# A two-layer trunk: the first layer's output projection in two parts, its memory attention three steps earlier, small matmuls in fewer groups

## The chip, the cores and the metric

The kernel runs on one core of a Trainium2 chip. TensorE (PE) multiplies matrices into PSUM, an accumulator memory of eight banks of 128 partitions x 512 fp32 values; VectorE (DVE), ScalarE (ACT) and GpSimd (POOL) do the elementwise work; DMA queues, here almost all issued by SyncE (SP), move data between device memory and the on-chip SBUF. Every engine works through its own list of instructions in order and waits on semaphores for the others. The metric is the device time of one execution in microseconds.

## The reference

One sequence of 512 tokens, model width 1024, two layers, all in float32. Each layer adds a token mixer and a memory cross-attention, which share one input and one output projection, and then a gated feed-forward block with a causal convolution of width 3:

```python
for i in range(DEPTH):
    h = rms_norm(x, attn_norm[i])
    if i % N_MIXERS == 0:
        proj = h @ w_in_diff[j]                  # 1024 -> 2560
        mix = diff_attention(q, k, v, ...)       # 6 heads of 2 x 64
    else:
        proj = h @ w_in_gla[j]
        mix = gla_attention(q, k, v, r, gate_low, ...)   # 4 heads, chunks of 64
    cross = memory_cross_attention(mem_q, mem, ...)      # 4 heads into 256 memory tokens
    x = x + jnp.concatenate([mix, cross], axis=-1) @ w_out[i]
    h = rms_norm(x, ffn_norm[i])
    x = x + conv_ffn(h, w_up[i], conv_w[i], conv_b[i], w_down[i])   # 1024 -> 5632 -> 1024
```

Differential attention normalizes queries and keys, adds a relative bias, masks by chunks, and subtracts a second softmax from the first: `w = p[:, :, 0] - lam * p[:, :, 1]`; its output is normalized per head. Memory attention normalizes the memory tokens, its queries and its keys, and is a plain softmax attention.

## The kernel before

**Products.** Every large product is made in three terms from operands split into a high and a low part (hi·hi, hi·lo, lo·hi), each a 128x128 weight against 512 columns; a 128x512 matmul follows the one before at 0.23 us. Weights come in pieces of up to 128x1024: a DMA into one of three raw buffers (`load_raw`, L208), a cast to the high part on ACT (`split_weights`, L201) and a subtraction for the low part on DVE (L202). There are five buffers each of high and low parts; `weights(key)` keeps two pieces made ahead. Activations are split in the same way by `split` (L234 on ACT, L235 on DVE), and memory-token operands too.

**Small work.** Between these run small fp32 matmuls: transposes (L170), the attention logits (L608 in the differential layer, L501 for memory) and values (L644, L534), and column sums (L342). PSUM banks are lent under four tags of two banks each: `lg` (logits, sums), `tp` (transposes), `mm` (large products), `sm` (values, second half of large products). A request for a bank waits until the last reader of its earlier use is done.

**Order.** PE's order is as written in the program. A queue `F` of large-product units stands beside it: `F.add(cost, unit)` or `gemm(...)` puts units in, `F.fill(us)` issues units for that much time, `F.need(mark)` issues all up to a mark, `F.flush()` all that is left. So the program writes the small groups and says with `F.fill` how much large work is put between them. The other engines' orders are made by a scheduler, except in the head (`with ... manual_schedule`, L351 to L425), where ACT, DVE, POOL and SP also follow the program.

**Head.** x is loaded and split in eight 128-row parts, each multiplied with the first weight piece as it arrives (L425) into four banks. At k = 6 the second piece is split (`make_piece(second)`: four casts and four subtractions), and the sums of squares are turned into r_x (`token_rsqrt`: L342 on PE, L184 on DVE, L191 and L192 on ACT, L177 to L179 on DVE). Then `halves` evacuates the four banks on ACT with the scale r_x into qs and ks (L560, L561).

**Differential layer** (`diff_layer`). `norms` makes the root-mean-square factors of qs and ks (squares L304, sums L305, multiplication L308), `prepare` transposes them (L170, evacuated at L584). A loop of 28 steps t handles unit t (head t // 4, query block t % 4) in stages one step apart: `logits(t)`, with the reduction L613, the exponentials L616 and the combination L622; `turn(t - 1)`, which transposes the weights through `tp` and copies them on ACT (L633); `values(t - 2)`. Every fourth step `finish` transposes and splits one head's output. `MemAttn` runs along it from step M0 = 12: `logits(b)` (maximum L504, exponentials L508, normalization L512 on POOL), `turn(u)` (copy on DVE, L521), `values(b)`; its `slot` picks which. `mem_kv(l)` makes a layer's memory operands, keys and values (L461, L462) and returns `operands` and `keys` (evacuation kmT at L470); that of layer 1 is made here as well, from t = 0. Two fills per step, each of `FA` = 3.0 us up to t = 13 and `FB` = 1.2 us after.

**Output projection.** `PASS` lists, for each layer, parts; each part is a list of column blocks c with the mixer rows k that it multiplies. Layer 0 has four: three inside the loop (t = 14, 20, 24), whose results `update` adds to x (L964 on DVE), and one after the loop, which also splits the new x and sums its squares (`squares`, L334 and L336) for the feed-forward block. `xT` is loaded again by `load_x` at t = 14, eight transfers of 256 KB.

**GLA layer** (`gla_layer`). Gates and decays (L795 to L802), then ten `slot`s of memory attention with `F.fill(2.4)` after each, then for each head h scores, turned keys, states and outputs with `F.fill(f)`, f = 2.5, between.

Of the kernel before, what the change touches and what calls it, by code (L numbers as in the profile page):

```python
# [22 lines left out]
NB = S // 128  # L23
# [106 lines left out]
def trunk(ctx, tc, head_d, x_t, mem_t, wpack, cols_a_d, cols_d, conv_d, gate_d, rel_bias, diff_lambda, consts, onehot, out):  # L130
# [224 lines left out]
    with tc.tile_pool(name="ini", bufs=1) as ip, tc.manual_schedule(engines={E.Activation, E.DVE, E.Pool, E.SP}):  # L355
# [50 lines left out]
        for k in range(KT):  # L406
            if k + 1 < KT:
                operands(k + 1)
            if k == 0:
                second.append(load_raw(raws[0], WTILE))  # L410
            if k == 4:
                bias_rows(rb, oh, bs)
            if k == KT - 2:
                make_piece(second)
                weights(("qk", 0))
                token_rsqrt("lg", acc[0], NB, r_x[:, 0])
                small_vectors()
                for c in range(2):
                    load(bias_d[:, 512 * c:min(512 * c + 512, 640)], bs[c])
            hi, lo = parts[k]  # L420
            terms = (xh[k], hi), (xh[k], lo), (xl[k], hi)
            todo = [(b, i) for b in range(NB) for i in range(3)]
            for b, i in sorted(todo, key=lambda bi: bi[1]) if k == 0 else todo:
                xp, w = terms[i]
                mm(first[b], xp[:, blk(b)], w, start=k == 0 and i == 0, stop=k == KT - 1 and i == 2)  # L425
# [16 lines left out]
        V.tensor_add(sq[:, 0:256], sq[:, 0:256], sq[:, 256:512])  # L442


    def mem_kv(l):
        hs, ls = [None] * KT, [None] * KT
        km = [None]

        def operands():
            if l == 0:  # L450
                mem_squares()
            km[0] = xtile().rearrange("p (b n) -> p b n", b=2)
            for k in range(KT):
                if k % 2 == 0:
                    mh, ml = split_tiles()
                c = blk(k % 2, 256)
                hs[k], ls[k] = mh[:, c], ml[:, c]
                split(hs[k], ls[k], memT[k // 2][:, c], c_mem(l, k))

        def ev(b, p):  # L460
            A.activation(km[0][:, b], p[:, :256], AF.Copy, scale=r_mem[:, b:b + 1])  # L461
            A.activation(vm[l][:, b], p[:, 256:], AF.Copy, scale=r_mem[:, b:b + 1])  # L462

        def keys():
            F.need(f"kv{l}")
            p = bank("lg")
            for hp in range(2):
                for b in range(2):
                    transpose(p[:, 256 * hp + 128 * b:256 * hp + 128 * b + 128], km[0][:, b, blk(hp)])
            A.activation(kmT[l].rearrange("p a b -> p (a b)"), p, AF.Copy, scale=c_mk(l))  # L470
        gemm(hs, ls, 2, ("kv", l), 512, ev,
             (lambda: token_rsqrt("lg", mem_acc[0], 2, r_mem)) if l == 0 else None)
        F.add(0.0, lambda: group_norm(None, km[0], 2, 4, 64))
        F.mark(f"kv{l}")
        return operands, keys


    class MemAttn:
# [36 lines left out]
        def turn(self, u):  # L515
# [5 lines left out]
            V.tensor_copy(pT, pt)  # L521
            self.live[u] = pT


# [15 lines left out]
        def slot(self, t):  # L540
            if t in (3, 5, 7, 9):
                self.values((t - 3) // 2)
            if t in (0, 2, 4, 6):
                self.logits(t // 2)
            if 0 <= t - 1 < 8:
                self.turn(t - 1)


    def diff_layer(pool, mix):
        r = r_x[:, 0]  # L550
        qm = pool.tile([128, NB, MEM], F32, name="qm", bufs=1)

# [119 lines left out]
        F.fill(1.2)  # L672
        prepare(1)
        ma = MemAttn(pool, 0, qm, mix, False)
        M0 = 12
        for t in range(28):
            if t == 0:
                project_qk(1)
                ops0, keys0 = mem_kv(0)
# [36 lines left out]
            if t % 4 == 3 and t >= 7:  # L716
                finish(t // 4 - 1)
        F.flush()


    def gla_layer(pool, mix, acc):
# [131 lines left out]
        def scores(h):  # L853
            pp = bank("lg")
            for b in range(NB):
                mm(pp[:, blk(b)], ke[:, blk(b)], qi[:, blk(b)], start=True, stop=True)
            V.copy_predicated(sv, MF.unsqueeze(1).to_broadcast([128, NB, 128]),
                              pp.rearrange("p (b n) -> p b n", b=NB))
            for b2 in range(2):
                pp = bank("lg")  # L860
                for b in (2 * b2, 2 * b2 + 1):
                    mm(pp[:, blk(b % 2, 192)], ki[:, blk(b)], qx[h][:, b], start=True, stop=True)
                pv = pp[:, :384].rearrange("p (b c n) -> p b c n", b=2, c=3)
                V.copy_predicated(
                    sv[:, 2 * b2:2 * b2 + 2].rearrange("p b (c n) -> p b c n", c=2),
                    MP.rearrange("p (c n) -> p c n", c=2).unsqueeze(1).to_broadcast([128, 2, 2, 64]), pv[:, :, 0:3:2])
                A.copy(sv[0:64, 2 * b2:2 * b2 + 2, 64:128], pv[0:64, :, 1])
                if b2 == 0:
                    F.fill(1.2)

        def turn_keys(h):
            pt = bank("tp")
# [47 lines left out]
                mix[t] = (mh, ml)  # L920
                F.fill(1.2)

        f = 2.5
        decays(0)
        F.need("qk")
        F.fill(f)
        products(0)
        F.fill(f)
        for h in range(4):
            scores(h)  # L930
            F.fill(f)
            turn_keys(h)
            if h < 3:
                decays(h + 1)
            F.fill(f)
            states(h, 0)
            F.fill(f)
            if h == 2:
                gate(0)
            outputs(h, 0)  # L940
            states(h, 1)
            if h < 3:
                products(h + 1)
            F.fill(f)
            outputs(h, 1)
            group_norm(pool, o_[h], NB, 1, 192, True)
            F.fill(f)
# [21 lines left out]
        squares(xT[n], acc, V if n == KT - 1 else eng)  # L969


    def tiles(l, part):
        cs, kk = [c for c, _ in PASS[l][part]], dict(PASS[l][part])
        if l == 0 and part == 3:
            return [2 * c + n for a in (0, 2) for n in range(2) for c in cs[a:a + 2]], kk
        return [2 * c + n for c in cs for n in range(2)], kk

    def out_proj(l, mix, part, acc):
        got = {}
        turns = cycle(("mm", "sm") if part == len(PASS[l]) - 1 else ("mm",))  # L980

        def unit(c, ks, n, i):
            if i == 0:
                if c not in got:
                    got[c] = weights(("o", l, part, c))
                got["p"] = bank(next(turns))
            p = got["p"]
            product(p, got[c], n, [mix[k] for k in ks], (i,))
            if i == len(ks) - 1:
                update(2 * c + n, p, None if acc is None else (lambda k: c_ffn(l, k)), acc, G if l else V)  # L990
        todo, kk = tiles(l, part)
        for n in todo:
            for i in range(len(kk[n // 2])):
                F.add(0.65, lambda n=n, i=i: unit(n // 2, kk[n // 2], n % 2, i))

    def ffn(pool, l, acc):
        rB = pool.tile([128, S], F32, name="rB", bufs=1)
# [1 line left out]
        for u in us:  # L999
            G.memset(u[:, 0:2], 0.0)  # L1000
        nu = [0]
        order = tiles(l, len(PASS[l]) - 1)[0]

        def up(parts, n):
            i = nu[0]
            nu[0] += 1
            p = bank("mm" if i % 4 < 2 else "sm")
            product(p, parts, n, list(zip(xh, xl)), order)
            return p, us[i % 4]

        def conv(p, u, j):
# [55 lines left out]
    for l in range(2):  # L1067
        with tc.tile_pool(name=f"at{l}", bufs=2) as pool:
            mix = [None] * 8
            if l == 0:  # L1070
                diff_layer(pool, mix)
            else:
                gla_layer(pool, mix, acc)
            acc = [None]
            out_proj(l, mix, len(PASS[l]) - 1, acc)
            F.flush()
        with tc.tile_pool(name=f"ff{l}", bufs=2) as pool:
            acc = ffn(pool, l, acc)

# [74 lines left out]
```

## Time and profile before

| quantity | value |
| --- | --- |
| runs of the kernel | 1201.24, 1201.85, 1203.02 us; median 1201.85 |
| profiled execution | 1205.09 us, span 1203.3 us, mean granted PE clock 0.997 |
| PE | 1186.3 us busy, 99% |
| DVE | 766.7 us, 64% |
| ACT | 542.4 us, 45% |
| POOL | 31.2 us, 3% |
| device memory | 112.65 MB read, 4.21 MB written, 97 GB/s over the span |

The span runs from the profile's first to its last instruction. In rows of the timeline stand the start in us, the duration, the engine with line and operation, output <- inputs, shapes, and in brackets the idle time of the engine before it with what ended it. Matmuls are pipelined: a row's duration overlaps the next row's start, so distances between starts say more than durations. In the list of costly groups stand line, engine, operation and count, then the total busy time in us and the mean in ns, then the engine's idle time before such instructions and what ended most of it; in the list of DMA issues, the count, the size of one, and the median us from issue to landing.

### The profile page before, as it was taken

Reading aid. Unit: us, or ns where it says so; the run is one execution under the profiler, and the core shown is the slowest. Engines: PE = TensorE matmul, PEld = TensorE weight load, DVE = VectorE, ACT = ScalarE, POOL = GpSimd, SP = SyncE. Lnnn points to the kernel's source line nnn. Section 1 sums busy time; section 2 is a strip of 40 time slices with the busy share of each in tenths; the row PEclk is TensorE's granted clock in tenths of the full one; section 3 lists DMA queues with packets and bytes.
Section 4 is the critical chain, followed back from the end, with each engine's and each line's share of the span. In section 5 each row is a group of like instructions: output and inputs, shape, how many; then the busy total and the mean of one; then the engine's idle time right before and its main releaser. Section 6 shows DMA issues by size and latency. Waiting matters only on the chain.

```text
span 1203.3 us, 14795 instructions
## 1 busy us (share of the span) xinstructions
PE 1186.3 (99%) x5656; PEld 967.9 (80%) x5656; DVE 766.7 (64%) x1280; ACT 542.4 (45%) x928; POOL 31.2 (3%) x45
## 2 busy tenths in 40 slices
PE   9999998999999999999999999999999999999998
PEld 7777776778888888888787788988888888888887
DVE  6567577887776533767447746768777653476741
ACT  6666666554444322434436534536544432243420
POOL 0000011000000000000020000003000000000000
PEclk9999999999999999999999999999999999999999
DMA  8333231133242322332442222143333232232231
GB/s 289 110 98 94 80 114 45 62 108 103 73 133 75 123 90 68 108 103 63 138 127 95 71 71 57 57 132 107 104 98 113 70 123 95 68 124 81 88 114 44
DMA packets 39556, 117.81 MB, mean 98 GB/s; under 512 B 4703, under 2 KB 6040, under 8 KB 39486
## 3 DMA queue, kind: packets, MB, share of 16 engines
q1 hardware_dynamic: 39342, 116.62, 30.1%
q8 instruction: 44, 0.72, 0.2%
q14 instruction: 26, 0.21, 0.1%
q10 hardware_dynamic: 144, 0.26, 0.1%
HBM read 112.65 MB, written 4.21 MB: 97 GB/s over the span
## 4 chain that ended last, share of the span: by engine, by line
PE 88%; DVE 6%; DMA 2%; ACT 2%; issue 1%; SPq 0%; DVEq 0%; ACTq 0%
PE ps_mm L269 8%; PE ps_mm L268 8%; PE ps_mm L270 8%; PE ps_sm L268 7%; PE ps_sm L269 7%; PE ps_sm L270 7%; PE ps_mm L251 5%; PE ps_mm L253 5%; PE ps_mm L252 5%; PE ps_tp L268 3%; PE ps_tp L269 3%; PE ps_tp L270 3%; PE ps_lg L269 3%; PE ps_lg L270 3%; PE ps_lg L268 3%; PE ps_tp L170 2%
## 5 line engine op out<-in xcount | busy, mean ns | idle before, releaser
L201 ACT CAST whi<-raw 128x1024 fp32r<-128x1024 f32 (+2 forms) x214 | 207.6, 977 | 247.3 <-PE ps_tp L269 133.9
L202 DVE TENSOR_TENSOR wlo<-raw,whi 128x1024 fp32r<-128x1024 f32 (+2 forms) x214 | 241.8, 1139 | 109.5 <-ACT whi L201 108.6
L268 PE MATMUL ps_mm<-xsh,whi 128*128 128x512 f32 x458 | 182.2, 398 | 0.2 <-DVE xt L964 0.2
L269 PE MATMUL ps_mm<-xsl,whi 128*128 128x512 f32 x458 | 179.1, 391 | 0.3 <-DVE xsl L235 0.2
L270 PE MATMUL ps_mm<-xsh,wlo 128*128 128x512 f32 x458 | 178.8, 390 | 0.0
L268 PE MATMUL ps_sm<-xsh,whi 128*128 128x512 f32 x374 | 145.5, 389 | 0.0
L269 PE MATMUL ps_sm<-xsl,whi 128*128 128x512 f32 x374 | 145.5, 389 | 0.0
L270 PE MATMUL ps_sm<-xsh,wlo 128*128 128x512 f32 x374 | 145.5, 389 | 0.0
L251 PE MATMUL ps_mm<-whi,xsh 128*128 128x512 f32 (+2 forms) x352 | 138.6, 394 | 1.8 <-ACT ks L561 1.7
L253 PE MATMUL ps_mm<-whi,xsl 128*128 128x512 f32 (+2 forms) x352 | 131.7, 374 | 0.3 <-DVE xsl L235 0.3
L252 PE MATMUL ps_mm<-wlo,xsh 128*128 128x512 f32 (+2 forms) x352 | 131.1, 372 | 0.0
L1014 ACT ACTIVATE cvo<-u,cv 128x512 f32<-128x512 f32 x88 | 71.6, 814 | 113.4 <-DVE u L1012 113.0
L269 PEld LDWEIGHTS ps_mm<-xsl,whi 128*128 128x128 f32 x458 | 86.3, 189 | 18.9 <-DVE xsl L235 1.5
L268 PEld LDWEIGHTS ps_mm<-xsh,whi 128*128 128x128 f32 x458 | 86.3, 188 | 18.5 <-DVE xt L964 0.9
L270 PEld LDWEIGHTS ps_mm<-xsh,wlo 128*128 128x128 f32 x458 | 86.3, 188 | 18.1
L1015 DVE SCALAR_TENSOR_TENSOR cvo<-u,cv,cvo 128x512 f32<-128x512 f32 x88 | 65.9, 749 | 31.6 <-ACT cvo L1014 31.4
L270 PEld LDWEIGHTS ps_sm<-xsh,wlo 128*128 128x128 f32 x374 | 70.2, 188 | 14.6
L269 PEld LDWEIGHTS ps_sm<-xsl,whi 128*128 128x128 f32 x374 | 70.2, 188 | 14.6
L268 PEld LDWEIGHTS ps_sm<-xsh,whi 128*128 128x128 f32 x374 | 70.2, 188 | 14.6
L251 PEld LDWEIGHTS ps_mm<-whi,xsh 128*128 128x128 f32 x352 | 66.7, 189 | 13.6 <-ACT ks L561 2.1
L253 PEld LDWEIGHTS ps_mm<-whi,xsl 128*128 128x128 f32 x352 | 66.4, 189 | 12.8 <-DVE xsl L235 0.5
L252 PEld LDWEIGHTS ps_mm<-wlo,xsh 128*128 128x128 f32 x352 | 66.7, 190 | 9.5
(257 smaller groups left out, 1767.6 us busy)
## 6 DMA issues: line engine op xcount, KB each, us to landing
raw<-in_wpack_dram SPq DMA_DIRECT2D x176, 512.0 KB, 3.5
raw<-in_wpack_dram SPq DMA_DIRECT2D x27, 256.0 KB, 3.5
xt<-in_x_t_dram SPq DMA_DIRECT2D x15, 256.0 KB, 6.0
xres<-xt SPq DMA_DIRECT2D x8, 256.0 KB, 2.8
xt<-xres SPq DMA_DIRECT2D x8, 256.0 KB, 3.1
out_dram<-xt SPq DMA_DIRECT2D x8, 256.0 KB, 2.0
bt<-bias_d SPq DMA_DIRECT2D x6, 256.0 KB, 4.1
raw<-in_wpack_dram SPq DMA_DIRECT2D x4, 384.0 KB, 3.0
```

The source lines that it names most:

```text
L170: nc.tensor.transpose(dst, src, ident[:n, :n])
L201: A.copy(hi[:, c], raw[:, c])
L202: V.tensor_sub(lo[:, c], raw[:, c], hi[:, c].bitcast(F32))
L251: mm(p, sh[k][:, blk(b)], hi, start=k == 0, stop=False)
L252: mm(p, sh[k][:, blk(b)], lo, start=False, stop=False)
L253: mm(p, sl[k][:, blk(b)], hi, start=False, stop=k == KT - 1)
L268: mm(p, hi[:, blk(n)], bh, start=i == first, stop=False)
L269: mm(p, hi[:, blk(n)], bl, start=False, stop=False)
L270: mm(p, lo[:, blk(n)], bh, start=False, stop=i == last)
L1014: A.activation(c, u[:, 2:], AF.Identity, scale=cv[l][:, 2, j:j + 1], bias=cv[l][:, 3, j:j + 1])
L1015: V.scalar_tensor_tensor(c, u[:, 1:S + 1], cv[l][:, 1, j:j + 1], c, op0=ALU.mult, op1=ALU.add)
```

## The change

- Layer 0's projection has two parts in place of four. Part 0 (rows 0, 1, 2) is queued at t = 16, part 1 (rows 3 to 7) at t = 26. Part 1 begins with the products of three output blocks without row 5, held open in three banks; the rest, with row 5, is queued after the loop, behind `finish(5)`.
- In the differential loop, the turn comes two steps and the values three steps after the logits; turns of both attentions stand together behind the logits; memory logits stand alone in mid-step; each step has two halves of one fill, 5.8, 2.6, 1.5 and 2.6 us by stages of t.
- Memory attention starts at M0 = 9; its queries' norm moves from t = 8 to t = 2, the queries from 11 to 4, the keys of layer 0 from 9 to 8. `mem_kv(1)` is created at t = 12 with a pool of its own for its split operands; its keys stay at t = 22.
- Every second copy of a memory turn in layer 0 is on ACT in place of DVE. The squares of layer 0's updates are summed on POOL in place of DVE, but for the last.
- In the head, `token_rsqrt` stands ahead of `make_piece(second)`.
- In the GLA layer, a fill of 2.5 us precedes memory attention, which has six steps with a fill of 4.0 in place of ten with 2.4; per head, both states, the next head's products and both outputs stand together, with f = 3.6.
- The feed-forward block takes its rows in plain order.

```diff
-FA, FB = 3.0, 1.2
+STEPS, FILL = (14, 19, 26), (5.8, 2.6, 1.5, 2.6)
...
-PASS = ([[(c, (0, 1)) for c in C4], [(c, (2, 3)) for c in C4], [(c, (6, 7)) for c in (0, 1)],
-         [(2, (6, 7, 4, 5)), (0, (4, 5)), (3, (6, 7, 4, 5)), (1, (4, 5))]],
+PASS = ([[(c, (0, 1, 2)) for c in C4], [(c, (3, 6, 7, 4, 5)) for c in C4]],
...
             if k == KT - 2:
+                token_rsqrt("lg", acc[0], NB, r_x[:, 0])
                 make_piece(second)
                 weights(("qk", 0))
-                token_rsqrt("lg", acc[0], NB, r_x[:, 0])
...
-            V.tensor_copy(pT, pt)
+            (V.tensor_copy if self.l or u % 2 == 0 else A.copy)(pT, pt)
...
-        M0 = 12
+        M0 = 9
         for t in range(28):
             if t == 0:
                 project_qk(1)
...
-                ops1, keys1 = mem_kv(1)
-            if t == 8:
-                ma.norm()
-            if t == 9:
-                keys0()
             if t == 2:
                 ops0()
-            if t == 11:
+                ma.norm()
+            if t == 12:
+                ops1, keys1 = mem_kv(1, pool, "mo", 8)
                 ops1()
             if t == 22:
                 keys1()
-            if t == 14:
+            if t == 16:
                 load_x(x_t)
                 out_proj(0, mix, 0, None)
-            if t in (20, 24):
-                out_proj(0, mix, t // 4 - 4, None)
-            f = FA if t < 14 else FB
-            if t == 11:
-                ma.queries()
+            if t == 26:
+                rest = out_proj(0, mix, 1, acc, 5)
+            f = FILL[bisect(STEPS, t)]
             if t < 24:
                 logits(t)
+            m = t - M0
+            if m in (4, 6, 8, 10):
+                ma.values(m // 2 - 2)
+            if 0 <= t - 3 < 24:
+                values(t - 3)
             if 0 <= t - 2 < 24:
-                values(t - 2)
-            F.fill(f)
+                turn(t - 2)
+            if 2 <= m < 10:
+                ma.turn(m - 2)
+            F.fill(f / 2)
             if t in (5, 6, 13, 14):
                 norms((t + 3) // 8, (t + 3) % 8)
-            if 0 <= t - 1 < 24:
-                turn(t - 1)
-            ma.slot(t - M0)
-            F.fill(f)
+            if t == 4:
+                ma.queries()
+            if t == 8:
+                keys0()
             if t in (7, 8, 15, 16):
                 prepare(2 * (t // 7) + (t + 1) % 8)
+            if m in (0, 2, 4, 6):
+                ma.logits(m // 2)
+            if t == 27:
+                F.flush()
+            F.fill(f / 2)
             if t % 4 == 3 and t >= 7:
                 finish(t // 4 - 1)
+        rest()
         F.flush()
...
-        for t in range(10):
-            ma.slot(t)
-            F.fill(2.4)
+        F.fill(2.5)
+        for t in range(6):
+            if 0 < t < 5:
+                ma.turn(2 * t - 2)
+                ma.turn(2 * t - 1)
+            if t > 1:
+                ma.values(t - 2)
+            if t < 4:
+                ma.logits(t)
+            F.fill(4.0)
...
+        f = 3.6
         for h in range(4):
             scores(h)
+            past_scores(h, 0)
             F.fill(f)
+            past_scores(h, 1)
             turn_keys(h)
             if h < 3:
                 decays(h + 1)
             F.fill(f)
             states(h, 0)
+            states(h, 1)
+            if h < 3:
+                products(h + 1)
             F.fill(f)
             if h == 2:
                 gate(0)
             outputs(h, 0)
-            states(h, 1)
-            if h < 3:
-                products(h + 1)
-            F.fill(f)
             outputs(h, 1)
...
-                update(2 * c + n, p, None if acc is None else (lambda k: c_ffn(l, k)), acc, G if l else V)
+                update(n, p, None if acc is None else (lambda k: c_ffn(l, k)), acc, G)
...
+        if late is None:
+            return give(units)
+        early = [u for u in units if u[0] < 4 and kk[u[0] // 2][u[1]] != late]
+        give([u for u in early if u[0] < 3])
+        return lambda: give([u for u in early if u[0] == 3] + [u for u in units if u not in early])
```

More of the change, by code (lines that the diff above doesn't have):

```diff
@@ L1 @@
 import math
+from bisect import bisect
 from collections import deque
@@ L442, in mem_squares, with mem_kv @@
         V.tensor_add(sq[:, 0:256], sq[:, 0:256], sq[:, 256:512])
-    def mem_kv(l):
+    def mem_kv(l, pool, tag, bufs):
         hs, ls = [None] * KT, [None] * KT
@@ L538, in values, with diff_layer @@
                 split(mh[:, blk(b)], ml[:, blk(b)], po[:, blk(hp)], 1.0)
[L540 to L549, printed above, removed]
+    def diff_layer(pool, mix, acc):
         r = r_x[:, 0]
@@ L678, in diff_layer @@
                 project_qk(1)
[L679 removed]
+                ops0, keys0 = mem_kv(0, xs, "xs", XS)
                 gemm(xh, xl, NB, ("v", 1), 512, lambda b, p: A.activation(
@@ L858, in scores, with past_scores @@
                               pp.rearrange("p (b n) -> p b n", b=NB))
[L859 to L869, printed above, removed]
+        def past_scores(h, b2):
+            pp = bank("lg")
+            for b in (2 * b2, 2 * b2 + 1):
+                mm(pp[:, blk(b % 2, 192)], ki[:, blk(b)], qx[h][:, b], start=True, stop=True)
+            pv = pp[:, :384].rearrange("p (b c n) -> p b c n", b=2, c=3)
+            V.copy_predicated(
+                sv[:, 2 * b2:2 * b2 + 2].rearrange("p b (c n) -> p b c n", c=2),
+                MP.rearrange("p (c n) -> p c n", c=2).unsqueeze(1).to_broadcast([128, 2, 2, 64]), pv[:, :, 0:3:2])
+            A.copy(sv[0:64, 2 * b2:2 * b2 + 2, 64:128], pv[0:64, :, 1])
         def turn_keys(h):
@@ L969, in update, with out_proj, unit @@
         squares(xT[n], acc, V if n == KT - 1 else eng)
[L972 to L982, printed above, removed]
+    def out_proj(l, mix, part, acc, late=None):
+        got, kk = {}, dict(PASS[l][part])
+        turns = cycle(("mm", "mm", "sm", "sm") if late is not None else ("mm", "sm") if acc else ("mm",))
+        def unit(n, i):
+            c, ks = n // 2, kk[n // 2]
             if i == 0:
@@ L985, in unit, with give @@
                     got[c] = weights(("o", l, part, c))
-                got["p"] = bank(next(turns))
-            p = got["p"]
-            product(p, got[c], n, [mix[k] for k in ks], (i,))
+                got["p", n] = bank(next(turns))
+            p = got["p", n]
+            product(p, got[c], n % 2, [mix[k] for k in ks], (i,))
             if i == len(ks) - 1:
-                update(2 * c + n, p, None if acc is None else (lambda k: c_ffn(l, k)), acc, G if l else V)
[L991 to L994, printed above, removed]
+                update(n, p, None if acc is None else (lambda k: c_ffn(l, k)), acc, G)
+        def give(units):
+            for u in units:
+                F.add(0.65, lambda u=u: unit(*u))
+        units = [(2 * c + n, i) for c, ks in PASS[l][part] for n in range(2) for i in range(len(ks))]
+        if late is None:
[3 more added lines that the diff above has]
+        return lambda: give([u for u in early if u[0] == 3] + [u for u in units if u not in early])
     def ffn(pool, l, acc):
@@ L1007, in up @@
             p = bank("mm" if i % 4 < 2 else "sm")
-            product(p, parts, n, list(zip(xh, xl)), order)
+            product(p, parts, n, list(zip(xh, xl)))
             return p, us[i % 4]
@@ L1069, in trunk @@
             mix = [None] * 8
+            sums, acc = acc, [None]
             if l == 0:
-                diff_layer(pool, mix)
+                diff_layer(pool, mix, acc)
             else:
[L1073 to L1076, printed above, removed]
+                gla_layer(pool, mix, sums)
+                out_proj(1, mix, len(PASS[1]) - 1, acc)
+                F.flush()
         with tc.tile_pool(name=f"ff{l}", bufs=2) as pool:
```

8 lines of the change are left out of this document (3 added, 5 removed).

## The prediction

> **What bounds the kernel now.** I read the engines' busy shares first, then PE's list of waits, then windows cut at each gap, and then the timeline round the gaps.
>
> ```profile
> span 1203.3 us, 14795 instructions
> PE 1186.3 (99%) x5656; PEld 967.9 (80%) x5656; DVE 766.7 (64%) x1280; ACT 542.4 (45%) x928; POOL 31.2 (3%) x45
> ```
>
> PE is busy for 99% of the span, and the diff leaves PE's list of 5330 programmed matmuls as it was: the same products, transposes and shapes in another order and in other banks. So no PE work can go away. What can change is the 17 us (1203.3 - 1186.3) in which PE stands still, what each restart costs, and the stretches at a lower clock. Some of this is beyond the change (the first load, the last output). The rest has names:
>
> ```profile
> PE ps_tp L170 <- DVE xt L521: 3.1, 2, 1.6
> PE ps_mm L251 <- ACT ks L561: 1.7, 1, 1.7
> PE ps_lg L501 <- DVE xt L800: 1.5, 1, 1.5
> ```
>
> These are the three largest that the change touches: what PE did, on whom it waited, microseconds in total, times, longest. The windows (length; PE busy; PEld, DVE, ACT, POOL; granted clock; DMA share; GB/s) say where they lie:
>
> ```profile
> core 0: us, PE busy (x) PEld busy (x) DVE busy (x) ACT busy (x) POOL busy (x), PEclk, DMA share, GB/s
> ...
> 110.00:180.00 70.00, 67.82 (x368) 53.33 (x367) 45.01 (x117) 43.52 (x111) 4.58 (x5) 1.00 0.25 81
> 180.00:195.00 15.00, 11.53 (x90) 8.90 (x89) 10.08 (x29) 11.11 (x30) 2.05 (x3) 1.00 0.27 79
> 195.00:199.00 4.00, 4.00 (x15) 3.23 (x15) 2.96 (x11) 2.34 (x7) 0.14 (x1) 0.57 0.02 7
> 199.00:243.00 44.00, 43.51 (x281) 33.82 (x281) 38.50 (x104) 22.84 (x67) 2.04 (x2) 1.00 0.19 59
> 243.00:272.00 29.00, 28.52 (x124) 22.27 (x123) 26.32 (x42) 16.97 (x26) 0.21 (x4) 1.00 0.36 112
> ...
> 659.00:663.00 4.00, 4.00 (x13) 2.77 (x12) 3.97 (x7) 3.94 (x11) 0.00 (x0) 0.57 0.00 0
> ```
>
> In the differential-attention loop PE idles 70.00 - 67.82 = 2.18, then 3.47, then 0.49 us: 6.1 in all. Twice the clock drops to 0.57 on average over a 4 us window: (1 - 0.57) x 4.00 = 1.7 us lost each time. Both follow a wait of 1.5 to 1.6 us (rows at 193.59 and 658.77 below). A wait costs more than the idle shown, too: in the head (below) the starts 30.08 and 32.18 lie 2.10 apart where products follow each other at 0.23, a loss of 1.87 with 1.71 shown. At about 0.1 more for each of some fourteen short waits, the loop loses 6.1 + 1.4 + 1.7 = 9.2 us.
>
> **The base.** The profiled execution took 1205.09 us, 1.8 around its span of 1203.3. It is 3.24 above the median of the runs, 1201.85. Terms below are differences made from profiled rows; I put them on the median, since nothing shows where in the span those 3.24 us lie.
>
> **The head.** `token_rsqrt` moves ahead of the four casts of the second weight piece.
>
> ```profile
> 23.92 0.95 PE L342 MATMUL ps_lg<-C,xt 128*128 128x1 f32 x8
> ```
> ```profile
> 30.04 0.26 ACT L191 ACTIVATE r_x<-ps_lg,eps 128x4 f32<-128x4 f32 x1 [1.36 <-DVE rs_v L184]
> ...
> 31.29 0.47 ACT L560 ACTIVATE qs<-ps_mm,r_x 128x256 f32<-128x256 f32 x1 [0.75 <-DMA raw<-in_wpack_dram]
> 31.66 0.47 ACT L561 ACTIVATE ks<-ps_mm,r_x 128x256 f32<-128x256 f32 x1
> ```
> ```profile
> 30.08 0.39 PE L425 MATMUL ps_sm<-whi,xsl 128*128 128x512 f32 x1
> 32.18 0.50 PE L251 MATMUL ps_mm<-whi,xsh 128*128 128x512 f32 x1 [1.71 <-ACT ks L561]
> ```
> ```profile
> L201 ACT CAST whi<-raw 128x1024 fp32r<-128x1024 f32 (+2 forms) x214 | 207.6, 977 | 247.3 <-PE ps_tp L269 133.9
> L202 DVE TENSOR_TENSOR wlo<-raw,whi 128x1024 fp32r<-128x1024 f32 (+2 forms) x214 | 241.8, 1139 | 109.5 <-ACT whi L201 108.6
> ...
> raw<-in_wpack_dram SPq DMA_DIRECT2D x176, 512.0 KB, 3.5
> raw<-in_wpack_dram SPq DMA_DIRECT2D x27, 256.0 KB, 3.5
> xt<-in_x_t_dram SPq DMA_DIRECT2D x15, 256.0 KB, 6.0
> ```
>
> The sums for r_x leave PE at 23.92 + 0.95 = 24.87, yet r_x starts only at 30.04: it stands behind the casts. Moved ahead, r_x is ready near 26.2, and if nothing else changed the evacuation that PE waits for (it ended at 31.66 + 0.47) would lie directly behind PE's last head product, 1.9 us sooner. But the order of instructions in the two built programs shows what takes its place. ACT, which runs its list in order, now has a fifth cast (the piece after the second) ahead of the first evacuation; before, that cast stood behind all eight. Its data are loaded into a raw buffer that the first subtraction of the second piece (L202) frees, and this subtraction now follows r_x: cast 1 from 25.4 to 26.4, subtraction to 27.6 (0.98 and 1.14 each), transfer issued then, landed at 27.6 + 3.5 = 31.1, fifth cast to 32.1, two evacuations 0.37 apart, the second taking 0.47: PE starts near 33.1 instead of 32.18, **+0.9**. Lower end: the cast also needs the high-half buffer that PE frees at 30.08 + 0.39, so it cannot end before 31.5, and PE starts at 32.4 or later: +0.3. Upper end: with 6.0 for the landing, as the row of x's loads has, +3.4. Idle at 33.1 is 2.6 us in place of 1.71, above the 1.5 that came before each half-clock stretch, so I add one stretch, **+1.7** (bounds 0 and 1.7). Queued behind that fifth cast are the evacuations, and behind them layer 0's first norms, which the 10 us of fill cover.
>
> The Trainium skill ("TensorE: Matmul & The Clock Gate", Part 1: The HAM clock gate) puts the drop to half rate after at least one idle window, about 3.4 us. By that a 2.6 us gap would cost no clock and the sum would be 1.7 lower; but here 1.5 to 1.6 us of idle stood ahead of both 0.57 windows, so the trace does not agree, and I go by the trace.
>
> **The differential loop.** What goes is the pair of waits in which the transposes of ks find their tp bank still held by a memory-attention turn:
>
> ```profile
> 183.15 0.60 PE L170 MATMUL ps_tp<-C,qs 128*128 128x128 f32 x4
> 185.27 0.66 PE L170 MATMUL ps_tp<-C,ks 128*128 128x128 f32 x4 [1.52 <-DVE xt L521]
> ...
> 191.38 0.60 PE L170 MATMUL ps_tp<-C,qs 128*128 128x128 f32 x4
> 193.59 0.66 PE L170 MATMUL ps_tp<-C,ks 128*128 128x128 f32 x4 [1.61 <-DVE xt L521]
> ```
> ```profile
> 180.93 1.20 DVE L308 TENSOR_TENSOR ks<-ks,rs_y 128x1024 f32<-128x1024 f32 x1
> ```
>
> With M0 = 9 and all turns placed behind the logits, these two and most of the short waits between 110 and 180 lose their place. But the same banks (two each of lg and tp) and the same in-order lists on ACT and DVE serve the new order, and I find a new wait at most steps where small groups meet: prepare(2)'s ks behind its 1.20 multiplication (1.0), logits(6) behind the memory's norm sums (0.6), logits(10) behind a cast between memory exponentials (0.4), ma.turn(1) behind finish(1)'s split of a tp bank (0.8), logits(14) (0.7), prepare(2)'s partner at t = 15 behind the 1.20 multiplication, itself behind a turn's copy (1.5), and at t = 16, where memory logits, two turns, finish(2) and prepare(3) meet: logits(16) (0.8), ma.turn(5) (0.5), qs behind an evacuation that stands behind a cast (0.8), ks behind the copy now put on ACT (0.8); logits(22) behind keys1 (0.2). The sum is 8.1. Each is bounded by 0 and by its releaser's own duration plus one cast (0.98) or multiplication: they sum to between 4 and 13. The t = 15 and 16 waits lie close enough for one half-clock stretch, 1.7. Taken: 9.8 against 9.2, **+0.6** (range -5 to +6).
>
> The four copies given to ACT and the six adds of squares given to POOL relieve DVE, which is idle often enough that this counts only in the tail. mem_kv(1) twelve steps later adds no work: its splits lie beside products. Its keys at t = 22 stand as before. `load_x` two steps later puts eight transfers of 256 KB on SP's list ahead of later weight pieces; DMA share is 0.25 and two pieces are kept ahead, so I take 0; without that cover, one landing of x, 6.0 us, less the step in between, about 2. The projection in two parts makes larger pieces (27 transfers of 256 KB become fewer), 12 fewer adds on DVE: 0 on PE.
>
> **Layer 0's tail.** Between 243 and 272 PE idles 0.48 us in five short waits, worth about 1.3 with restarts, while DVE is busy 26.32 of 29.00. The new tail holds n = 0..2 open in three banks and has twelve products of n = 3 to run while finish(5) is split, and half a dozen fewer adds on DVE. I take 0.3 left, **-1.0** (0 to -1.3; a loss if POOL's adds end late is in the second rival's range).
>
> **The GLA layer.** A fill of 2.5 now stands ahead of the memory logits.
>
> ```profile
> 658.77 1.54 PE L501 MATMUL ps_lg<-kmT,xt 64*128 64x256 f32 x6 [1.50 <-DVE xt L800]
> ```
> ```profile
> 659.81 1.28 ACT L173 ACT_TABLE_LOAD   x1
> ```
>
> The 1.50 wait and its half-clock stretch, 3.5 with the restart, are covered by 2.5 us of products. Late next are the turns, which need the exponentials behind the table load of 1.28: 1.1 remains (0.5 to 1.5). At the end one group, with less fill left for it, loses 0.3 more. Net **-2.1** (-3.0 to -0.5).
>
> **Fewer groups.** About 103 groups of small matmuls between large ones become 80 in the built order. Entering one:
>
> ```profile
> 710.29 0.39 PE L253 MATMUL ps_mm<-whi,xsl 128*128 128x512 f32 x1
> 710.52 0.60 PE L170 MATMUL ps_tp<-C,q 128*96 128x128 f32 x4
> 710.95 0.60 PE L170 MATMUL ps_tp<-C,k 128*96 128x128 f32 x4
> 711.31 0.47 PE L251 MATMUL ps_mm<-whi,xsh 128*128 128x512 f32 x1
> 711.62 0.39 PE L252 MATMUL ps_mm<-wlo,xsh 128*128 128x512 f32 x1
> ```
>
> From 710.29 to 711.62 is 1.33; two product slots of 0.23 and eight transposes at 0.43 for four leave 0.01. So a group costs 0.01 to 0.02, and 23 fewer save **-0.25** (0 to -0.5).
>
> **The sum**: 0.9 + 1.7 + 0.6 - 1.0 - 2.1 - 0.25 = -0.15; 1201.85 - 0.15 = 1201.7 us. Waits trade places.
>
> **Rivals.** (A) *The waits go and few come back: faster.* For it: the waits at 185, 193 and 658 have a definite cause that the new order removes, and fills of 2.6 us or more then lie ahead of most groups. Against it: ACT busy 11.11 of 15.00 and DVE 10.08 exactly there. With half the loop's loss (-4.6), the head at its lower end without a clock stretch (+0.3), tail and GLA as above: 1201.85 - 4.6 + 0.3 - 1.0 - 2.1 - 0.25 = 1194.2.
>
> (B) *In-order lists at t = 15 and 16: slower.* Place: ACT's weight casts and copies standing ahead of evacuations while both tp banks are held. Price: the loop's waits at their upper end of 13, with two clock stretches of 1.7 instead of one, 16.4 - 9.2 = +7.2; with the head's +2.6 and the other terms 1201.85 + 7.2 + 2.6 - 3.35 = 1208.3. It decides once two of those waits exceed 1.5 us. For it: both such waits did so before. Against: more fill between them.
>
> (C) *It does not do what it says.* The filler runs dry ahead of part 1 of the projection, so that small groups run uncovered as before and only the head's loss remains: 1201.85 + 2.6 - 0.25 = 1204.2.
>
> **Chances.** A difference under 0.2% (2.4 us) counts as none. Forecast 0.36: its own range is 1198 to 1206, so 0.22 within, 0.06 faster, 0.08 slower. A 0.31, faster. B 0.29, slower. C 0.04, half within, half slower. Faster 0.37, same 0.24, slower 0.39. A spreads from 1190 to 1199 and B from 1204 to 1214 by the ends of their terms; a tenth left out at each side, a third of A and of B, gives 1193 to 1211, and I take 1191.5 below, since the loop's own lower end (-5) lies beyond A's -4.6.
>
> **What would show it.** Right: PE's wait on ks in the head longer than 1.71; no wait of L170 on L521 over 1 us in the loop, but several of 0.5 to 1.5 at t = 15 and 16; the GLA's 1.50 gone with its 0.57 window. Wrong: the first product after the head starting before 32.2; the loop's idle under 3 or over 10 us; PE's busy time without clock stretches moving by more than 1 us.

## The result, and the profile after

The changed kernel takes 1213.53 us (median of 4 runs, 1212.01 to 1214.33), the kernel before 1202.43 (4 runs, 1201.24 to 1203.02): a ratio of 1.0092, 95% interval 1.0075 to 1.0110. It is 11.1 us slower, above the range's upper end of 1211. Its profiled execution took 1212.01 with a span of 1210.2 and a mean granted clock of 0.994, against 1205.09, 1203.3 and 0.997: only 6.9 between the two profiles. The other 4.2 us matter below.

PE's list of waits after the change (what it did, on whom it waited, total, times, longest):

```profile
PE ps_mm L251 <- ACT ks L554: 2.9, 1, 2.9
PE ps_tp L170 <- DVE ks L308: 2.3, 1, 2.3
PE ps_mm L269 <- DVE xsl L235: 2.3, 2, 1.9
PE ps_tp L170 <- ACT xt L626: 2.0, 2, 1.3
PE ps_tp L170 <- DVE xsl L235: 1.7, 3, 1.1
PE ps_tp L170 <- DVE rcd L612: 1.6, 1, 1.6
PE ps_tp L170 <- ACT xt L521: 1.5, 1, 1.5
PE ps_mm L268 <- ACT xsh L234: 1.4, 1, 1.4
```

None of the three waits that led the list before is there in its old form; these eight lines are. In order of time they are the head (2.9), the transposes of ks for `prepare(2)` (2.3), steps 15 and 16 of the loop (0.7, 1.6, 1.3, 1.5), as the third and the eighth line the last rows of the new x at the start of the feed-forward block (row 6: 0.3; row 7: 1.4 for its high part and 1.9 for its low part), and, as the longest part of the fifth line, a group of transposes at the end of the GLA layer (1.1). The windows (columns as in the prediction) show what came after the head, after `prepare(2)`, after step 15 and after row 7:

```profile
34.00:38.00 4.00, 4.00 (x12) 3.09 (x12) 2.29 (x5) 4.00 (x12) 0.00 (x0) 0.57 1.04 399
...
112.00:116.00 4.00, 4.00 (x14) 3.19 (x13) 1.49 (x7) 1.37 (x2) 0.00 (x0) 0.57 0.03 13
...
191.00:195.00 4.00, 4.00 (x17) 2.71 (x14) 2.44 (x7) 2.31 (x9) 0.80 (x2) 0.57 0.60 214
...
280.00:284.00 4.00, 4.00 (x10) 2.56 (x9) 1.77 (x3) 1.32 (x2) 0.00 (x0) 0.60 0.28 113
```

Four stretches at about half clock, 1.6 to 1.7 us lost in each, where before had two.

PE's work is the same in both, so the start of one and the same instruction tells what was lost up to it. The first product after the head starts 0.84 later than before (33.02 against 32.18), the column sums of the feed-forward block 7.86 later (279.56 against 271.70). Adding up PE's start-to-start distances less the usual distance for each shape, by stages, gives after against before: up to 45 us +2.4, 45 to 160 +3.0, 160 to 245 -0.7, 245 to 300 +4.8, then -1.0 to 620, -2.4 in the first part of the GLA layer (to 720) and +0.7 from there on: 6.8 of the 6.9.

### The profile page after: what moved, and what is told of

Its sections match the earlier page's. It is cut to its first block, busy times and chain, and to the rows that moved or that the text cites. A ratio compares the mean times of both kernels' runs of the same rounds, so it can differ in the third digit from the quotient of the medians.

```text
span 1210.2 us, 14755 instructions
## 1 busy us (share of the span) xinstructions
PE 1186.6 (98%) x5656; PEld 970.0 (80%) x5656; DVE 763.4 (63%) x1256; ACT 543.5 (45%) x930; POOL 42.1 (3%) x51
## 4 chain that ended last, share of the span: by engine, by line
PE 89%; DVE 5%; ACT 3%; DMA 1%; issue 1%; DVEq 0%; ACTq 0%
PE ps_mm L269 8%; PE ps_mm L270 8%; PE ps_mm L268 8%; PE ps_sm L269 7%; PE ps_sm L268 7%; PE ps_sm L270 7%; PE ps_mm L251 5%; PE ps_mm L253 5%; PE ps_mm L252 5%; PE ps_lg L269 3%; PE ps_lg L268 3%; PE ps_lg L270 3%; PE ps_tp L268 3%; PE ps_tp L269 3%; PE ps_tp L270 3%; PE ps_tp L170 2%
## 5 line engine op out<-in xcount | busy, mean ns | idle before, releaser
L201 ACT CAST whi<-raw 128x1024 fp32r<-128x1024 f32 (+4 forms) x212 | 207.8, 984 | 261.7 <-PE ps_tp L269 134.7
L202 DVE TENSOR_TENSOR wlo<-raw,whi 128x1024 fp32r<-128x1024 f32 (+4 forms) x212 | 246.9, 1168 | 115.9 <-ACT whi L201 114.6
L268 PE MATMUL ps_mm<-xsh,whi 128*128 128x512 f32 x446 | 176.9, 397 | 1.4 <-ACT xsh L234 1.4
L270 PE MATMUL ps_mm<-xsh,wlo 128*128 128x512 f32 x446 | 174.1, 390 | 0.0
L268 PE MATMUL ps_sm<-xsh,whi 128*128 128x512 f32 x386 | 150.4, 390 | 0.0
L269 PE MATMUL ps_sm<-xsl,whi 128*128 128x512 f32 x386 | 150.3, 389 | 0.0
L270 PE MATMUL ps_sm<-xsh,wlo 128*128 128x512 f32 x386 | 150.3, 389 | 0.0
L251 PE MATMUL ps_mm<-whi,xsh 128*128 128x512 f32 (+2 forms) x336 | 130.4, 388 | 2.9 <-ACT ks L554 2.9
L253 PE MATMUL ps_mm<-whi,xsl 128*128 128x512 f32 (+2 forms) x336 | 126.1, 375 | 0.3 <-DVE xsl L235 0.3
L252 PE MATMUL ps_mm<-wlo,xsh 128*128 128x512 f32 (+2 forms) x336 | 125.8, 374 | 0.0
```

The lines of the kernel that those rows point to most:

```text
L201: A.copy(hi[:, c], raw[:, c])
L202: V.tensor_sub(lo[:, c], raw[:, c], hi[:, c].bitcast(F32))
L251: mm(p, sh[k][:, blk(b)], hi, start=k == 0, stop=False)
L252: mm(p, sh[k][:, blk(b)], lo, start=False, stop=False)
L253: mm(p, sl[k][:, blk(b)], hi, start=False, stop=k == KT - 1)
L268: mm(p, hi[:, blk(n)], bh, start=i == first, stop=False)
```

## The experiments

**The tail's sums on DVE again.**

```diff
-                update(n, p, None if acc is None else (lambda k: c_ffn(l, k)), acc, G)
+                update(n, p, None if acc is None else (lambda k: c_ffn(l, k)), acc, G if l else V)
```

> After, with the squares of layer 0's updates summed on DVE again. Theory P (POOL's six additions stretch the DVE instructions that run beside them, and so delay the last rows' low parts): the waits of 1.44 and 1.94 us on rows 6 and 7 of x fall below 0.6 each, the DVE subtractions beside them return to 0.75 us, the half-clock stretch after 281 us goes: 4 to 6 us faster than after, about 1208. Theory R (the last rows are late because the projection's last part ends with whole rows and casts of later weights stand ahead of them): DVE has six additions more ahead of the same rows; waits as in after or longer: 1213 to 1215.

Measured: 1205.42, ratio 1.0026 (1.0016 to 1.0036). Eight microseconds of the eleven hang on this one choice of engine. Both lines on the last rows are gone from the list (the 1.44 and the 1.94 of the expectation are both row 7's), and DVE's end of the tail now reads

```profile
272.57 1.22 DVE L202 TENSOR_TENSOR wlo<-raw,whi 128x1024 fp32r<-128x1024 f32 x1
273.71 0.74 DVE L235 SCALAR_TENSOR_TENSOR xsl<-xt,cols,xsh 128x512 fp32r<-128x512 f32 x1
```

where after had (DVE, then POOL, then PE of the changed kernel; start, duration):

```profile
268.00 1.79 DVE L235 SCALAR_TENSOR_TENSOR xsl<-xt,cols,xsh 128x512 fp32r<-128x512 f32 x1
269.71 2.31 DVE L202 TENSOR_TENSOR wlo<-raw,whi 128x1024 fp32r<-128x1024 f32 x1
271.94 0.68 DVE L972 TENSOR_TENSOR xt<-xt,ps_sm 128x512 f32<-128x512 f32 x1
...
274.81 3.44 DVE L202 TENSOR_TENSOR wlo<-raw,whi 128x1024 fp32r<-128x1024 f32 x2
278.17 0.74 DVE L235 SCALAR_TENSOR_TENSOR xsl<-xt,cols,xsh 128x512 fp32r<-128x512 f32 x1
```
```profile
267.39 1.85 POOL L336 TENSOR_TENSOR xt<-xt 128x512 f32<-128x512 f32 x1 [3.52 <-ACT xt L334]
269.47 1.46 POOL L336 TENSOR_TENSOR xt<-xt 128x512 f32<-128x512 f32 x1 [0.23 <-ACT xt L334]
275.05 2.12 POOL L336 TENSOR_TENSOR xt<-xt 128x512 f32<-128x512 f32 x1 [4.11 <-ACT xt L334]
```
```profile
276.51 0.50 PE L268 MATMUL ps_mm<-xsh,whi 128*128 128x512 f32 x1 [1.44 <-ACT xsh L234]
278.96 0.50 PE L269 MATMUL ps_mm<-xsl,whi 128*128 128x512 f32 x1 [1.94 <-DVE xsl L235]
```

Each of the three POOL additions has a DVE instruction beside it that takes about 1 us more than its usual 0.75 or 1.22. DVE works through its list in order, so it falls behind: PE issued row 6's last product at 265.92 and the projection's last one at 269.32, but the addition of row 6's update starts only at 271.94, and row 7's low part comes last.

**The same step done to before.** In before, `acc, G if l else V` becomes `acc, G`:

> Before, with the squares of layer 0's updates summed on POOL, all but the last. Theory P: DVE instructions beside POOL's additions take 1.5 to 2 times as long in the tail and PE's wait at the end of it (0.17 us) grows past 1 us: 1 to 4 us slower than before. Theory R: DVE is relieved of six additions of 0.68 us, and the wait stays or goes: 0 to 0.5 us faster.

Measured: 1208.12, ratio 1.0046 (1.0031 to 1.0061), 5.5 us slower, somewhat more than expected. In its list PE now waits on L235, where before had 0.17:

```profile
PE ps_mm L269 <- DVE xsl L235: 2.3, 2, 2.1
```

So the cost does not need the new projection.

**POOL adds for nobody.** To tell POOL's presence from the sums' passing through it, e1 was given six additions whose results nothing reads:

```diff
+                if l == 0 and acc and 0 < n < KT - 1:
+                    z = xtile()
+                    G.tensor_add(z, xT[n], xT[n])
```

> e1 (after with the squares on DVE), and POOL makes six additions of the same shape beside them whose results nothing reads. Theory P1 (DVE instructions are held up while POOL adds): DVE's subtractions for x's last rows again take 1.5 us or more, PE waits over 1 us for rows 6 or 7, and the time returns most of the way from e1's 1205.4 to after's 1213.5, to 1209 or more. Theory P2 (POOL is merely slow, and the chain of sums through it is what came late): no reader waits for POOL, so 1205 to 1206.

Measured: 1212.82, ratio 1.0076 (1.0060 to 1.0093). P2 falls: no instruction waits for these additions, and DVE's subtractions and PE's waits return (DVE, POOL and PE of this kernel):

```profile
274.47 1.52 DVE L235 SCALAR_TENSOR_TENSOR xsl<-xt,cols,xsh 128x512 fp32r<-128x512 f32 x1
```
```profile
273.55 1.89 POOL L996 TENSOR_TENSOR xt<-xt 128x512 f32<-128x512 f32 x1 [4.29 <-DVE xt L972]
```
```profile
276.05 0.50 PE L269 MATMUL ps_mm<-xsl,whi 128*128 128x512 f32 x1 [0.71 <-DVE xsl L235]
278.00 0.49 PE L268 MATMUL ps_mm<-xsh,whi 128*128 128x512 f32 x1 [1.22 <-ACT xsh L234]
279.04 0.50 PE L269 MATMUL ps_mm<-xsl,whi 128*128 128x512 f32 x1 [0.55 <-DVE xsl L235]
```

In the profiles the tail accounts for 3.4 of the 6.4 us between this kernel and e1; 1.0 more is lost in the head and 1.9 from 620 us on. Both are places with more time at half clock: the windows 32 to 36 and 36 to 40 have a clock of 0.50 and 0.66 where e1 has 0.72 and 0.85, and 640 to 644 and 644 to 648 have 0.86 and 0.71 where e1 has 1.00; why stays open. So this run shows the mechanism, and not that it is worth the whole 8 us. (Its undisturbed additions are also shorter, 1.04 us against 1.35.)

**The head.** After with `token_rsqrt` behind `make_piece(second)`:

```diff
-                token_rsqrt("lg", acc[0], NB, r_x[:, 0])
                 make_piece(second)
                 weights(("qk", 0))
+                token_rsqrt("lg", acc[0], NB, r_x[:, 0])
```

> After, with token_rsqrt behind make_piece(second) as in before. Theory of the prediction (a fifth cast, waiting for its transfer, stands ahead of the first evacuation): PE's wait in the head goes from 2.9 back to 1.7 us and the half-clock stretch at 34 us goes: 2.4 us faster than after, about 1211. Rival (the wait is the transfer's own and stays): within 0.5 of after, 1213.5.

Measured: 1207.66, ratio 1.0048 (1.0033 to 1.0063): 5.9 us faster than after, not 2.4. And the opposite edit in before:

> Before, with token_rsqrt ahead of make_piece(second) alone. Theory H (the fifth cast ahead of the first evacuation makes PE wait 2.9 us, followed by a half-clock stretch, where before's usual execution waits not at all): 4 to 6 us slower than before, about 1207. Rival (before's profiled head with its 1.71 us wait is the usual one): 2.4 us slower, about 1204.7.

Measured: 1207.29, ratio 1.0029 (1.0015 to 1.0043). PE waits in the head as it does after the change:

```profile
PE ps_mm L251 <- ACT ks L561: 3.0, 1, 3.0
```

The direction is H's. The medians lie 4.7 us apart, the ratio's 3.5 us lies below H's 4 to 6, and its interval covers the rival's 2.4 as well. What the rival rests on is answered by profiles instead: the squares-on-POOL kernel has before's head unchanged, and there PE starts

```profile
29.74 0.39 PE L425 MATMUL ps_sm<-whi,xsl 128*128 128x512 f32 x1
30.15 0.50 PE L251 MATMUL ps_mm<-whi,xsh 128*128 128x512 f32 x1
```

with no wait at all. In before's own profile the fourth cast waited 5.20 us for its transfer, here 4.54 from an earlier start, and ran 2.0 us sooner. In the nine profiles with `token_rsqrt` late PE's wait lies anywhere from 0 to 1.7; in the five with it early it is 2.8 to 3.0 each time. Before's profile has the longest of the nine, so the rival's condition falls, and the prediction's base had the 1.7 us in it by chance.

**The norms a step earlier.** `norms` of all four of qs and ks, at t = 4, 5, 12, 13:

> After, with the four norms of qs and ks one step earlier. Theory N (the chain of ks's norm stands in ACT's and DVE's lists behind casts, subtractions and head 0's own norm, and ends 2.3 us too late for prepare(2); the same norm chain is late at t = 15): the 2.3 wait and its half-clock stretch at 112 us go, and the 1.6 wait on ks at 189 us falls: 4 to 6 us faster than after, about 1208.5. Rival (the whole list moves with it, and head 0's norm is then late): the wait appears at another group, within 1 us of after.

Measured: 1212.31, ratio 1.0091 (1.0070 to 1.0113): about after's 1.0092, which is the rival's outcome. The 2.3 wait is gone and the stage from 45 to 160 us loses 4.3 less, but 160 to 245 loses 4.0 more:

```profile
190.29 0.66 PE L170 MATMUL ps_tp<-C,qs 128*128 128x128 f32 x4 [2.44 <-ACT xt L626]
191.72 1.12 PE L170 MATMUL ps_tp<-C,ks 128*128 128x128 f32 x4 [0.78 <-ACT qT L577]
196.68 0.48 PE L601 MATMUL ps_lg<-kT,qT 64*128 64x128 f32 x2 [1.09 <-ACT xt L508]
```

**Both dear edits undone.** Squares on DVE and `token_rsqrt` late:

> After, with the squares on DVE and token_rsqrt behind make_piece(second). If the two costs are independent (tail 8.1 and head 5.9 below after's 1213.5, as measured one by one), the time is 1199.5, some 3 us below before; if they share half-clock stretches, up to 1203.

Measured: 1202.34, ratio 0.9999 (0.9988 to 1.0010). The two account for the whole loss; undone together they give 11.2 us, less than 8.1 + 5.9, though by the intervals of the ratios that difference is not clear of noise. All the rest of the change, loop, projection, GLA and groups, comes to nothing in sum.

**The second pair's norms alone early**, on top of that (t = 4 and 5, the third pair's left at 13 and 14):

> c1 with the norms of the second pair of heads alone (t = 5 and 6) one step earlier; those of the third pair stay. With all four moved, the loop's first half lost 4.3 us less and its second half 4.0 us more in the profile. If the two halves are separate, 4 us faster than c1, about 1195.5; if the second half is slower because the first is faster, no difference to c1.

Measured: 1200.37, ratio 0.9983 (0.9974 to 0.9993): half of the expected gain.

**The copies of memory turns back on DVE**, on top of that:

```diff
-            (V.tensor_copy if self.l or u % 2 == 0 else A.copy)(pT, pt)
+            V.tensor_copy(pT, pt)
```

> c2 (after with squares on DVE, token_rsqrt late, the second pair's norms a step earlier) with all copies of memory turns on DVE. If ACT's list at t = 15 and 16 is what the move of copies filled (the wait of 1.8 us on such a copy), that wait goes and c2's 1200.4 falls by 1 to 2. If DVE is as crowded there, the wait is on DVE's copy instead, as in before (1.5 and 1.6 us), and the time stays within 1 us of c2.

Measured: 1198.61, ratio 0.9970 (0.9961 to 0.9979), 1.8 us below c2 and 3.6 below before: the fastest version here. (c2 was run in another set; the two ratios' intervals overlap at their ends.) The time is the first theory's and the place the second's: the wait on the copy moves to DVE and is shorter (1.34 after 1.8):

```profile
192.33 0.66 PE L170 MATMUL ps_tp<-C,qs 128*128 128x128 f32 x4 [2.24 <-ACT xt L626]
194.33 0.63 PE L170 MATMUL ps_tp<-C,ks 128*128 128x128 f32 x4 [1.34 <-DVE xt L521]
```

**GLA: the fill alone, in before.**

```diff
+        F.fill(2.5)
         for t in range(10):
             ma.slot(t)
```

> Before, with a fill of 2.5 us ahead of the GLA layer's memory attention. Theory of the prediction (the 1.5 us wait on the gates' chain and its half-clock stretch are covered): 2 to 3.5 us faster than before, about 1199.5. Rival (the products are only taken from later fills, and the wait comes back where they lack): within 1 us of before.

Measured: 1202.30, ratio 1.0000 (0.9990 to 1.0009): the rival. The wait on the gates is gone, and the turns and values wait instead:

```profile
663.15 0.63 PE L170 MATMUL ps_tp<-C,xt 128*128 128x128 f32 x4 [1.45 <-DVE xt L512]
672.11 1.09 PE L534 MATMUL ps_sm<-xt,vm 128*64 128x128 f32 x14 [0.80 <-DVE xt L521]
```

**GLA's whole new order alone, in before:**

> Before, with the GLA layer's new order alone (fill of 2.5, memory attention in six steps, larger groups). The fill alone gave nothing, since the waits came back at the turns. Theory: with turns in pairs and fills of 4.0 ahead of them the waits of 0.8 to 1.5 there shrink, but the last group of transposes waits 0.9 longer: -1 to +0.5 us. Rival (fewer groups pay): 2 us or more faster.

Measured: 1201.08, ratio 0.9992 (0.9983 to 1.0001): about 1 us faster, at the edge of the theory's -1 to +0.5 us, and not the rival's 2 us or more for fewer groups.

**The projection in two parts alone, in before**, with before's loop (the squares stay on DVE):

> Before, with the output projection of layer 0 in two parts alone (squares on DVE, the feed-forward rows in plain order, loop otherwise as before). Theory of the prediction for the tail without POOL: five short waits between 243 and 272 us go: 1 to 1.5 us faster than before. Rival: the loop of before lacks the work that parts 0 to 2 gave it from t = 14, and small groups run uncovered: 1 to 5 us slower.

Measured: 1206.38, ratio 1.0040 (1.0026 to 1.0054), the rival. The tail loses nothing (PE is busy for 29.00 of 29.00 us from 243 to 272), but the loop, which had parts 0 to 2 to put between its groups, now waits there, longest in this row:

```profile
194.07 1.34 PE L500 MATMUL ps_lg<-kmT,xt 64*128 64x256 f32 x8 [2.90 <-DVE nmd L612]
```

## Why the prediction was wrong

**The step that failed** stands in two sentences of it: that the squares given to POOL "relieve DVE, which is idle often enough that this counts only in the tail", and for the tail "-1.0 (0 to -1.3; a loss if POOL's adds end late is in the second rival's range)". It counted half a dozen additions (0.68 us each) off DVE and did not ask what POOL's additions do to the DVE instructions beside them; the loss that it allowed for was POOL's sums ending late, and PE waited at most 0.4 us for those. In the profile the tail lost 4.8 us more than before's, and when the additions went back to DVE the runs were 8.1 us shorter. (Of the profiles, after's is its fastest run and e1's its slowest, so they lie closer than the medians.) Without POOL the sentence on the tail was right: e1 has no wait there, and loses 1.4 us less than before.

**Its signs** did not look there. Those of being right nearly all came: 2.89 in the head, waits of 0.7 to 1.6 at t = 15 and 16, no wait and no half-clock window where the GLA layer had them. One failed, a wait of 1.54 on the copy of a memory turn. None of being wrong came: PE idled 8.2 us between 110 and 243, within the bounds of 3 and 10. So the signs spoke for a prediction that was off by 11 us.

**The head's mechanism was right, and its size was short.** A start at 33.1 was predicted, behind the fifth cast and its transfer, with a half-clock stretch after it. The changed kernel's ACT and PE:

```profile
24.76 0.26 ACT L191 ACTIVATE r_x<-ps_lg,eps 128x4 f32<-128x4 f32 x1 [6.77 <-DVE rs_v L184]
...
31.09 1.04 ACT L201 CAST whi<-raw 128x1024 fp32r<-128x1024 f32 x1 [2.04 <-DMA raw<-in_wpack_dram]
```
```profile
33.02 0.50 PE L251 MATMUL ps_mm<-whi,xsh 128*128 128x512 f32 x1 [2.89 <-ACT ks L554]
```

But +2.6 was measured against a profiled head with a wait of 1.71, the longest of the nine. Set against no wait, 2.9 and a stretch of 1.6 make 4.5, between b2's 3.5 and e2's 5.9.

**The base.** The prediction left the 3.24 us between before's profile and its median unassigned and took terms from that profile. Likely places can be named: up to 1.7 us in the head, and one half-clock stretch too many. A stretch that costs 1.7 of 1203 us lowers the mean clock by 0.0014; before's profile has two and a mean of 0.997. Of the 27 runs of before beside the second set of experiments eight had 1.000, seven 0.999, seven 0.998 and five 0.997, so a run in the middle had about one, by this estimate. Terms that take away a stretch were counted in full where the median may hold it in part. The median's run has no trace, so this is argued and not shown.

**GLA** is such a case in part: -2.1 predicted and -1.7 in the profiles, as much as the stretch at 659; by the runs 0.0 for the fill and 0.08%, about 1 us, for the whole order. The turns that were named as late next (1.1) waited 1.45 with the fill alone and 0.3 in the changed kernel, but its last group of transposes, priced at 0.3 more, waited 1.1 where before had 0.4. The stretch is not the whole account: with the fill alone the clock was 1.000 in eight of ten runs, and the time stayed the same. The new waits then cost about what the stretch had; no run separates the two.

**The loop**: +0.6 predicted, +2.3 in the profiles (+3.0 - 0.7). The places were mostly right: ks at t = 7 (predicted 1.0, measured 2.3 and a stretch), at t = 15 ks (1.5; 1.57), at t = 16 qs (0.8; 1.30) and ks (0.8; 1.54), the last behind a copy put on ACT; undoing that move was worth 1.8, in a kernel with the second pair's norms earlier. One stretch was allowed for, and two came.

**Fewer groups**: no run shows a gain from them; nothing contradicts 0.01 us a group.

**The rivals.** B's time, 1208.3, came nearest, and its waits at t = 15 and 16 are there; but it was not what made the kernel slower, since with the loop as changed and the two dear edits undone the time is before's. That the measured time lies in B's spread, 1204 to 1214, is luck.

## What to carry to other kernels

An operation moved to a less busy engine is not off the busy one's path: look for what the two share, and price the neighbours' stretched durations, above all in the last chain before a stage that has nothing else to run. Before a profile's waits are used as terms, compare its time with the median and place the difference; waits that hang on a transfer's landing and half-clock stretches come and go between executions. And moving a short chain ahead of a long one moves what the long one frees, here a buffer that the next transfer was waiting for.

## What the runs showed of the hardware

DVE instructions that read two SBUF operands are held up when they start while POOL adds, by up to about a microsecond each. Over the changed kernel the subtraction of 128x1024 takes 1.23 us alone (167 of them) and 1.22 when it starts before POOL's instruction (4); of the five that start while POOL adds, four take 1.61 to 2.31, and the fifth starts 0.05 before the addition ends. The subtraction for a row of x (128x512, both operands in SBUF) takes 0.75 alone (11) or when it starts first (8), and 1.78 to 1.79 when POOL has started first (5). The late subtractions of 128x1024 all end 1.1 us after POOL's addition does, so DVE waits for POOL's end and does nearly all of its work behind it. The additions of an update, which read one operand from PSUM, keep 0.68 us when they start beside POOL (4 of them, in the GLA layer's projection; the longest 0.68). The Trainium skill ("SBUF — State Buffer", Who interferes with whom) says that a DVE instruction with two SBUF inputs contends with a GpSimd instruction that reads SBUF, and that one with at most one SBUF input, outside the modes that use two ports, does not. In the section "SBUF: two separate sides" of that page the Trainium skill says that whichever starts first gets the shared pair of ports for the whole instruction while the other fully blocks. This case agrees in all three, with the numbers above.

A gap of PE of some 1.5 us was enough for a stretch at half clock in some executions and not in others. Five profiles have before's pair of waits in the loop, 1.5 and 1.6 us: in three a stretch follows (before, `token_rsqrt` early, the GLA fill alone), in two it does not (squares on POOL, the GLA order alone). The last of these, row and window:

```profile
192.96 0.66 PE L170 MATMUL ps_tp<-C,ks 128*128 128x128 f32 x4 [1.61 <-DVE xt L521]
```
```profile
194.00:198.00 4.00, 4.00 (x39) 3.20 (x36) 3.32 (x11) 3.16 (x11) 0.50 (x1) 1.00 0.06 20
```

After the head's gap of 2.8 to 3.0 us a stretch came in all five profiles that have it. In the kernel with POOL's idle additions one (a clock of 0.58 from 643 to 647) follows waits of only 0.46 and 0.21 us, so the length of a single gap does not decide it alone.
